# Attention with cosine similarity, 96 heads: the second pair's K squared and scaled in halves, no transposes by DMA, one dummy fewer, new orders on four engines

## The chip, the cores and the metric

The kernel runs on one core of a Trainium2 chip. What counts is the device time of one execution in microseconds (us), as the median of several runs. The engines are TensorE (PE, whose weight loads are listed as PEld), VectorE (DVE), ScalarE (ACT), GpSimd (POOL) and SyncE (SP), which here only issues DMAs. Each works through a list of its own in order, and they meet through semaphores.

## The reference

```
Q, K, V: (8, 12, 512, 64) float32;  tau = 0.1
Q_norm = Q / (norm(Q, axis=-1) + 1e-10)
K_norm = K / (norm(K, axis=-1) + 1e-10)
scores = einsum('bhqd,bhkd->bhqk', Q_norm, K_norm) / tau
weights = softmax(scores, axis=-1)
out = einsum('bhqk,bhkd->bhqd', weights, V)      float32
```

There are 8 x 12 = 96 heads, each with 512 queries and 512 keys of 64 numbers.

## The kernel before

Two heads form a pair, and the program is a loop over 48 pairs, numbered 0 to 47. Every step of a pair is put into a table with a name, an engine and the names of the steps it needs. The names are used below:

- LD.s.0 and LD.s.1 load Q and K of pair s (256 KB each), LV.s loads V, ST.s stores the result. All are issued by SP, but for the first K halves.
- SQ.s squares Q and K. Most pairs do this on POOL in one step of 1024 numbers per partition; pair 0 by quarters, pair 1 Q on ACT and K on DVE (512 each), pair 2 on POOL in two steps.
- SSQ.s adds the squares up in eight matmuls with an identity, and RED.s finishes this on DVE. Pair 0 does without the matmuls.
- The factor 1 / norm comes for pairs 0 to 2 from a logarithm and exponentials on ACT (LN.s, EX.s), later from small Newton steps on DVE (NEW.g.k, group g of one or two pairs).
- SCL.s.0 and SCL.s.1 multiply Q and K by these factors and write bf16 into `qn`; Q on DVE, K mostly on POOL.
- TR.s transposes `qn` on PE with an identity (16 small matmuls for a pair), and EVA.s copies the result from PSUM to `qt` on DVE. Pairs 0 and 1 do this in parts (TR.s.w, with w = 0 for Q and 1 for K). For seven pairs (9, 15, 21, 27, 33, 39, 45) K goes instead by a DMA that transposes, XT.s.1, which SP issues once SCL.s.1 is done; PE then transposes Q alone (8 matmuls), and the copy is half as wide.
- SCO.s.c computes the scores of a chunk of 128 keys for both heads (two matmuls of 512 columns) into one half of a PSUM tile of two halves, `scps`; EXP.s.c takes the exponential of the chunk on ACT (1024 numbers per partition), into `et`. So SCO may be at most two chunks ahead of EXP.
- VC.s turns V into bf16 on POOL, with a column of ones beside it. PV.s.h.t multiplies the exponentials with it (32 matmuls a pair); the column of ones gives the sum of the weights. RCP.s and NRM.s divide by it on DVE.

The buffers are rings: 18 pairs of `qk`, 6 of `vf`, 5 of `qn` and `qt`, 3 of `et`, 8 of `ob`. Several steps share three PSUM banks, named x, o0 and o1; who takes a bank waits for its last user by the order in PE's list.

The order of the work on each engine isn't decided by a planner: the table ORDER at the end of the file holds five written lists, one for each engine, and an engine does its list word for word. A step that waits holds up all that stands behind it on its engine. This counts on SP too: a store, a transposing DMA or a load into a ring place that isn't free yet holds up all loads behind it.

At the start PE has nothing to do until the first loads are there. It runs WARM = 19 dummy matmuls from the beginning, and FILL = (4, 0) more behind the first transposes (`fill`, line 639).

Of the kernel before, what the change touches and what calls it, by code (L numbers as in the profile page):

```python
# [5 lines left out]
ACT = mybir.ActivationFunctionType  # L6
# [118 lines left out]
def bass_cosine_similarity_attention_kernel(  # L125
# [127 lines left out]
    def sums(s, dst, free):  # L253

        sqs = [k for k in (("SQ", s, 0), ("SQ", s, 1)) if k in P.ops]
# [33 lines left out]
    def scaled(s, w, eng, r, needs):  # L289
        iqn, iq = s % R_QN, s % R_QK  # L290
        r = r.rearrange("p (h t) -> p h t", h=2).unsqueeze(3).to_broadcast([128, 2, NT, DIM])
# [3 lines left out]
        P.add(("SCL", s, w), eng, needs + [key("XT", p, w), key("TR", p), key("TR", p, w), *(key("TR", p, w, h) for h in range(2))],  # L295
              lambda e: e.tensor_tensor(out=o, in0=x, in1=r, op=ALU.mult))  # L296

    def transposed(s, name, blocks, dst, needs, **kw):
# [6 lines left out]
        P.add(name, "pe", needs + ["eye"], tr, **kw)  # L305

    def head():
# [13 lines left out]
        for h in range(2):  # L321
# [4 lines left out]
            for w in range(2):  # L326
# [4 lines left out]
                def tr(e, w=w, h=h, hs=hs):  # L331
# [6 lines left out]
                P.add(("EVA", 0, w, h), "dve", [("TR", 0, w, h)], lambda e, w=w, hs=hs: e.tensor_copy(  # L338
                    out=qt[0][hs, w], in_=tp[w][hs]))
# [80 lines left out]
    def pair(s):  # L420
# [14 lines left out]
        if s:  # L435
            gone = [key("RED", s - R_SQ, *y) for y in ((0,), (1,), (0, 0), (0, 1), (1, 0), (1, 1))]
            if s in SQ_ON:
                for w in range(2):
                    squares(s, engine(SQ_ON[s][w], "SQ", s, w), (w,), 512 * w, 512 * w + 512, [("LD", s, w)] + gone)
            else:  # L440
                squares(s, "pool", (0,), 0, 1024, [("LD", s, 0), ("LD", s, 1)] + gone)
        if 0 < s < LOGS:
# [7 lines left out]
                [("SCL", s - 1, 1)] if engine("pool", "SCL", s - 1, 1) == "dve" else [])  # L450
# [3 lines left out]
            scaled(s, 1, eng, r, [("EX", s, 0), ("EX", s, 1)])  # L454
# [42 lines left out]
        ready = [key("EVA", s), key("EVA", s, 0), key("EVA", s, 1), key("XT", s, 0), key("XT", s, 1)]  # L497
# [4 lines left out]
        for c in range(NT) if s else ():  # L502
# [14 lines left out]
            P.add(("SCO", s, c), "pe", [("SCO", *chunks[i - 1]) if i else None, *ready, scores_read(i - 2)], sco)  # L517
# [33 lines left out]
        for h in range(2) if s not in CHUNKED else ():  # L551
            for t in range(NT):
                def pv(e, h=h, t=t):
                    for c in range(NT):
# [10 lines left out]
                       *([("EVA", 1, 1), ("EVA", 0, 1, 1)] if s == 0 else [])], pv,  # L565
# [78 lines left out]
    if FILL[1]:  # L644
# [13 lines left out]
FILL = (4, 0)  # L658
# [10 lines left out]
        LD.0.0.0 LD.0.0.1 LD.1.0 LD.1.1 LD.2.0 LD.2.1 LD.3.0 LD.3.1 LV.0 LD.4.0 LD.4.1 LD.5.0 LD.5.1 LD.6.0 LV.1  # L669
        LD.6.1 LD.7.0 LD.7.1 LD.9.1 LD.9.0 LV.2 LV.3 LV.5 LD.8.1 LD.8.0 LV.4 LD.13.0 LD.15.0 LV.7 LD.11.1 LD.10.0  # L670
        LD.10.1 LD.11.0 LV.6 LV.8 LD.16.0 LD.14.1 ST.1 LD.12.0 LD.12.1 LD.13.1 LD.15.1 ST.4 XT.9.1 LD.18.0 LV.9
        LD.14.0 LV.10 LD.21.0 ST.0 LD.17.0 LV.14 LV.11 LD.16.1 LD.19.0 ST.5 ST.3 LD.24.0 LD.17.1 ST.2 LV.12 LV.15
        LD.18.1 LD.27.0 ST.6 LD.20.0 LV.13 LD.19.1 LD.23.0 LD.20.1 XT.15.1 LV.17 LV.16 LD.21.1 LD.24.1 LD.23.1 ST.7
# [167 lines left out]
```

## Time and profile before

| what | value |
|---|---|
| three timed runs | 191.36, 192.54, 193.3 us |
| their median | 192.54 us |
| the profiled execution | 191.03 us |
| its span, from the first to the last instruction | 189.2 us |
| granted TensorE clock | 1.000 |
| HBM read, written | 37.75 MB, 12.58 MB |
| DMA, mean over the span | 273 GB/s |

The page and the views of the trace describe the one profiled execution. An engine is busy while it computes; issuing DMAs and waiting on semaphores don't count. A group of instructions is given with its line in the code, engine and operation, then output and inputs, their shapes and the number of instructions; behind the bar its busy time in us, the mean duration of one in ns, and how long the engine was idle just ahead of such instructions and what ended that. Instructions of one engine overlap at their edges, so the mean duration is longer than the busy time divided by the count. Lines of the kernel before and after differ by up to 15 from the middle of the file on.

### The profile page before, as it was taken

To read this page: it belongs to the slowest core of one execution; us is meant where nothing else is said; L and a number is where in the kernel's file an instruction comes from. 1 tells how busy PE (TensorE), PEld (TensorE's weight loads), DVE (VectorE), ACT (ScalarE), POOL (GpSimd) and SP (SyncE) were. 2 spreads that over 40 slices of the span, in tenths; PEclk is the share of its full clock that TensorE was granted. 3 is DMA by queue.
4 is the path that set the end of the run, shared out by engine and by line. 5 is a ranking of instruction groups with operands and counts; after the bars stand their busy time and mean duration, and the time that the engine had idled before them with its cause. 6 is when DMAs were issued, how large, how long until landed. Compare 5 with 4: busy or idle time off the path is not lost.

```text
span 189.2 us, 7234 instructions
## 1 busy us (share of the span) xinstructions
PE 174.0 (92%) x3023; PEld 110.2 (58%) x3023; DVE 146.1 (77%) x451; ACT 181.3 (96%) x209; POOL 160.1 (85%) x147
## 2 busy tenths in 40 slices
PE   7999998999998999998898999999999999988893
PEld 5455664665665565665565656565656666654542
DVE  2999988879887977878798688876869877697424
ACT  5599999999999999999999999999999999999992
POOL 1599999999999999999999999999899998355100
PEclk9999999999999999999999999999999999999999
DMA  5999999579999999999999999999999570938423
GB/s 151 335 349 349 348 350 368 175 234 310 361 359 251 309 353 346 314 254 349 376 373 303 241 343 299 352 255 281 294 318 328 132 243 22 309 90 170 132 93 116
DMA packets 56257, 51.73 MB, mean 273 GB/s; under 512 B 6944, under 2 KB 56224, under 8 KB 56224
## 3 DMA queue, kind: packets, MB, share of 16 engines
q1 hardware_dynamic: 55792, 50.93, 86.4%
q8 instruction: 24, 0.39, 0.9%
q10 hardware_dynamic: 432, 0.33, 0.6%
q14 instruction: 9, 0.07, 0.1%
HBM read 37.75 MB, written 12.58 MB: 266 GB/s over the span
## 4 chain that ended last, share of the span: by engine, by line
ACT 84%; PE 6%; DVE 4%; POOL 2%; DMA 2%; issue 0%; ACTq 0%; DVEq 0%
ACT et L527 80%; ACT et L523 2%; DMA qk<-in_K_dram 2%; PE bps L268 2%; PE scps L512 1%; POOL qn L296 1%; PE scps L359 1%; POOL sq L250 1%; DVE qt L490 1%; PE bps L555 1%; PE bps L484 1%; DVE qn L296 1%; DVE qn L327 1%; ACT et L364 1%; PE bps L333 0%
## 5 line engine op out<-in xcount | busy, mean ns | idle before, releaser
L527 ACT ACTIVATE et<-scps 128x1024 bf16<-128x1024 f32 x184 | 168.9, 1168 | 0.2 <-PE scps L512 0.2
L250 POOL TENSOR_TENSOR sq<-qk 128x1024 bf16<-128x1024 f32 (+2 forms) x48 | 87.3, 1830 | 6.0 <-DMA qk<-in_Q_dram 5.7
L512 PE MATMUL scps<-qt 64*128 64x512 bf16 x376 | 74.1, 386 | 8.5 <-ACT et L527 7.2
L555 PE MATMUL bps<-vb,et 128*128 128x65 bf16 x1472 | 66.4, 194 | 0.0
L555 PEld LDWEIGHTS bps<-vb,et 128*128 128x128 bf16 x1472 | 51.8, 98 | 24.5 <-issue 16.2
L296 POOL TENSOR_TENSOR qn<-qk,rk 128x512 bf16<-128x512 f32 x44 | 45.3, 1042 | 9.4 <-DVE rk L398 5.7
L490 DVE COPY qt<-bps 128x1024 bf16<-128x1024 bf16 (+1 forms) x46 | 29.9, 650 | 10.9 <-PE bps L484 10.0
L296 DVE TENSOR_TENSOR qn<-qk,nps 128x512 bf16<-128x512 f32 x50 | 33.8, 681 | 0.5
L571 DVE TENSOR_TENSOR ob<-bps,rd 128x512 f32<-128x512 f32 x47 | 32.5, 692 | 1.1
L512 PEld LDWEIGHTS scps<-qt 64*128 64x128 bf16 x376 | 18.3, 93 | 25.9 <-ACT et L527 14.3
L268 PE MATMUL bps<-sq,ident 128*128 128x128 bf16 x376 | 29.1, 220 | 0.5 <-POOL qn L296 0.5
L532 POOL TENSOR_SCALAR vb<-vf 128x512 bf16<-128x512 f32 x48 | 29.5, 625 | 0.0
L268 PEld LDWEIGHTS bps<-sq,ident 128*128 128x128 bf16 x376 | 21.1, 98 | 11.0 <-issue 8.1
L569 DVE RECIPROCAL rd<-bps 128x8 f32<-128x8 f32 x47 | 9.7, 207 | 18.7 <-PE bps L555 15.2
L484 PE MATMUL bps<-ident,qn 64*128 64x64 bf16 x680 | 17.9, 191 | 1.4 <-DVE nps L276 0.3
L484 PEld LDWEIGHTS bps<-ident,qn 64*128 64x128 bf16 x680 | 13.2, 95 | 7.8 <-DVE nps L276 3.4
L276 DVE TENSOR_REDUCE nps<-bps 128x16 f32<-128x128 f32 x45 | 13.4, 297 | 2.1 <-PE bps L268 2.1
L390 DVE TENSOR_TENSOR nps<-nps,ys 128x32 f32<-128x32 f32 (+1 forms) x48 | 9.1, 192 | 1.0
L394 DVE SCALAR_TENSOR_TENSOR nps<-nps,ys 128x32 f32<-128x32 f32 (+1 forms) x48 | 9.1, 191 | 0.7
L237 PE MATMUL scps<-warm_in 128*128 128x256 bf16 x23 | 4.8, 394 | 1.1 <-DVE warm_in L232 1.1
L398 DVE SCALAR_TENSOR_TENSOR nps<-nps,ys 128x16 f32<-128x16 f32 (+1 forms) x25 | 4.3, 177 | 0.5
L402 DVE TENSOR_SCALAR ys<-nps 128x32 int32<-128x32 int32 (+1 forms) x24 | 4.4, 181 | 0.4
(45 smaller groups left out, 46.8 us busy)
## 6 DMA issues: line engine op xcount, KB each, us to landing
vf<-in_V_dram SPq DMA_DIRECT2D x48, 256.0 KB, 5.4
qk<-in_Q_dram SPq DMA_DIRECT2D x47, 256.0 KB, 5.9
qk<-in_K_dram SPq DMA_DIRECT2D x47, 256.0 KB, 6.0
out_dram<-ob SPq DMA_DIRECT2D x47, 256.0 KB, 4.5
qk<-in_Q_dram SPq DMA_DIRECT2D x2, 128.0 KB, 2.6
qk<-in_K_dram ACTq DMA_DIRECT2D x2, 128.0 KB, 2.8
out_dram<-ob SPq DMA_DIRECT2D x1, 128.0 KB, 2.3
qt<-qn SPq DMA_TRANSPOSE x7, 3.5
```

The source lines that it names most:

```text
L250: emit = lambda e: e.tensor_tensor(out=b, in0=a, in1=a, op=ALU.mult)
L268: last = e.matmul(out=ps[:, 0:128], lhsT=ident[:, :], rhs=sq[s % R_SQ][:, :, 8 * k : 8 * k + 8], start=(k == 0), stop=(k == 7))
L276: lambda e: e.tensor_reduce(out=dst(None), in_=ps[:, 0:128].rearrange("p (w g e) -> p w g e", w=2, e=8), axis=AX.X, op=ALU.add))
L296: lambda e: e.tensor_tensor(out=o, in0=x, in1=r, op=ALU.mult))
L484: last = e.transpose(t_ps[:, k, b, :], qn[s % R_QN][ks, b // NT, b % NT].rearrange("p h d -> p (h d)"), ident[ks, ks])
L490: lambda e, lo=lo, hi=hi: e.tensor_copy(out=qt[iqt][:, :].rearrange("p w t (k x) -> p k (w t) x", k=2)[:, :, lo:hi], in_=t_ps[:, :, lo:hi]))
L512: last = e.matmul(out=sc_ps[:, 2 * b + k, :], lhsT=qt[iqt][64 * h : 64 * h + 64, 1, n, :], rhs=qt[iqt][64 * h : 64 * h + 64, 0, :, :], sta ...
L527: lambda e, c=c, b=b: e.activation(out=et[iet][:, c, :, :], in_=sc_ps[:, 2 * b : 2 * b + 2, :], func=ACT.Exp, scale=scale, bias=bias))
L532: lambda e: e.tensor_scalar(out=vb[:, iq, :, :, 0:DIM].rearrange("p c h d -> p h c d"), in0=vf[iv][:, :, :].rearrange("p h (c d) -> p h c ...
L555: last = e.matmul(out=o_ps[:, h, 65 * t : 65 * t + 65], lhsT=et[iet][:, c, h, 128 * t : 128 * t + 128], rhs=vb[:, iq, c, h, :], start=(c = ...
L569: lambda e: e.reciprocal(out=rd[io][:, :], in_=grid[:, :, :, DIM]))
L571: lambda e: e.tensor_tensor(out=ob[io][:, :], in0=grid[:, :, :, 0:DIM], in1=rd[io][:, :].unsqueeze(3).to_broadcast([128, 2, NT, DIM]), op= ...
```

## The change

There are five edits.

1. K of pair 1 is squared in two steps, one for each head: the first head (256 numbers per partition) on DVE as SQ.1.1.0, the second on ACT as SQ.1.1.1, right behind Q's square. Before, DVE did all 512. SSQ.1 needs all three.
2. K of pair 1 is scaled (SCL.1.1.0, SCL.1.1.1), transposed (TR.1.1.0, TR.1.1.1) and copied (EVA.1.1.0, EVA.1.1.1) in two halves of 256 keys. The second half uses the bank o0. The chunks SCO.1.0 and SCO.1.1 need the first half of K alone, SCO.1.2 and SCO.1.3 the second too.
3. No pair is transposed by DMA any more (`XT = {}`); PE transposes Q and K of all pairs, in 16 matmuls, with the copy of full width.
4. FILL goes from (4, 0) to (3, 0): three late dummies.
5. The lists of SP, POOL, DVE and PE are new. ACT's list is as before but for SQ.1.1.1.

```diff
-        sqs = [k for k in (("SQ", s, 0), ("SQ", s, 1)) if k in P.ops]
+        sqs = [k for k in (("SQ", s, 0), ("SQ", s, 1), ("SQ", s, 1, 0), ("SQ", s, 1, 1)) if k in P.ops]
...
-    def scaled(s, w, eng, r, needs):
+    def scaled(s, w, eng, r, needs, part=(), ts=slice(0, NT)):
         iqn, iq = s % R_QN, s % R_QK
...
-        o = qn[iqn][:, w].rearrange("p t h d -> p h t d")
-        x = qk[iq][:, w].rearrange("p h (t d) -> p h t d", t=NT)
+        o = qn[iqn][:, w, ts].rearrange("p t h d -> p h t d")
+        x = qk[iq][:, w].rearrange("p h (t d) -> p h t d", t=NT)[:, :, ts]
...
+    def copied(name, needs, dst, src_):
+
+        eng = engine("dve", *name)
+        P.add(name, eng, needs, (lambda e: e.activation(out=dst, in_=src_, func=ACT.Copy)) if eng == "act"
+              else lambda e: e.tensor_copy(out=dst, in_=src_))
...
     def second():
 
-        tp = [b[:, 0:256].bitcast(bf16).rearrange("p (t x) -> p t x", t=NT) for b in (x_ps, o_ps[:, 1])]
-        for w in range(2):
-            transposed(1, ("TR", 1, w), range(NT * w, NT * w + NT), tp[w],
-                       [("SCL", 1, w)] + ([("RED", 1, 0)] if w else []),
-                       take=["o1" if w else "x"], until=("EVA", 1, w))
-            P.add(("EVA", 1, w), "dve", [("TR", 1, w)],
-                  lambda e, w=w: e.tensor_copy(out=qt[1][:, w], in_=tp[w]))
+        banks = {"x": x_ps, "o1": o_ps[:, 1], "o0": o_ps[:, 0]}
+        for w, j, bank in ((0, None, "x"), (1, 0, "o1"), (1, 1, "o0")):
+            lo, hi = (0, NT) if j is None else (2 * j, 2 * j + 2)
+            tp = banks[bank][:, 0:256].bitcast(bf16).rearrange("p (t x) -> p t x", t=NT)[:, 0 : hi - lo]
+            part = (w,) if j is None else (w, j)
+            transposed(1, ("TR", 1, *part), range(NT * w + lo, NT * w + hi), tp,
+                       [("SCL", 1, *part)] + ([("RED", 1, 0)] if j == 0 else []) + ([("TR", 1, 1, 0)] if j else []),
+                       take=[bank], until=("EVA", 1, *part))
+            copied(("EVA", 1, *part), [("TR", 1, *part)], qt[1][:, w, lo:hi], tp)
...
-            P.add(("SCO", s, c), "pe", [("SCO", *chunks[i - 1]) if i else None, *ready, scores_read(i - 2)], sco)
+            P.add(("SCO", s, c), "pe", [("SCO", *chunks[i - 1]) if i else None, *ready, key("EVA", s, 1, 1) if c > 1 else None,
+                                      scores_read(i - 2)], sco)
...
-SQ_ON = {1: ('act', 'dve'), 2: ('pool', 'pool')}
+SQ_ON = {1: (('act',), ('dve', 'act')), 2: (('pool',), ('pool',))}
...
-XT = {9: (1,), 15: (1,), 21: (1,), 27: (1,), 33: (1,), 39: (1,), 45: (1,)}
+XT = {}
...
-FILL = (4, 0)
+FILL = (3, 0)
...
     "act": """
-        LD.0.1.0 LD.0.1.1 table SQ.0.0.0 SQ.0.1.0 SQ.0.1.1 LN.0.0 EX.0.0 LN.0.1 EX.0.1 SQ.1.0 EXP.0.0.0 EXP.0.0.1 LN.1
+        LD.0.1.0 LD.0.1.1 table SQ.0.0.0 SQ.0.1.0 SQ.0.1.1 LN.0.0 EX.0.0 LN.0.1 EX.0.1 SQ.1.0 SQ.1.1.1 EXP.0.0.0
...
```

How the lists move is seen at three places. The first is DVE's row at the start of the program, from the scaling of pair 0's first head on. In it `qn0` and `qt0` belong to pair 0, `sq1`, `xs1` and `qn1` to pair 1, `xs2` to pair 2; the lines with `COPY qt0` are EVA.0. Before:

```order
L327 TENSOR_TENSOR qn0<-qk0,bps 128x4x64 x2
L318 TENSOR_REDUCE xs0<-sq0 128x4
L338 COPY qt0<-bps 64x512
L327 TENSOR_TENSOR qn0<-qk0,nps 128x4x64
L338 COPY qt0<-bps 64x512
L250 TENSOR_TENSOR sq1<-qk1 128x512
L327 TENSOR_TENSOR qn0<-qk0,nps 128x4x64
L338 COPY qt0<-bps 64x512
L276 TENSOR_REDUCE xs1<-bps 128x16
L338 COPY qt0<-bps 64x512
L296 TENSOR_TENSOR qn1<-qk1,nps 128x2x4x64 x2
L276 TENSOR_REDUCE xs2<-bps 128x16
```

The same stretch of DVE's row after the change:

```order
L333 TENSOR_TENSOR qn0<-qk0,bps 128x4x64 x2
L324 TENSOR_REDUCE xs0<-sq0 128x4
L311 COPY qt0<-bps 64x512 x2
L333 TENSOR_TENSOR qn0<-qk0,nps 128x4x64
L250 TENSOR_TENSOR sq1<-qk1 128x256
L333 TENSOR_TENSOR qn0<-qk0,nps 128x4x64
L311 COPY qt0<-bps 64x512
L276 TENSOR_REDUCE xs1<-bps 128x16
L311 COPY qt0<-bps 64x512
L296 TENSOR_TENSOR qn1<-qk1,nps 128x2x2x64
L296 TENSOR_TENSOR qn1<-qk1,nps 128x2x4x64
L296 TENSOR_TENSOR qn1<-qk1,nps 128x2x2x64
```

The two copies of the first head stand side by side, where a scaling of the second head stood between them; the square is half as wide; and K of pair 1 is scaled in two pieces around Q.

The second place is PE's row in the same stretch; `sq1`, `sq2` and `sq3` mark the sums of pairs 1 to 3, `qt0` and `qt1` the scores of pairs 0 and 1, `warm_in` the dummies. Before:

```order
L333 MATMUL bps<-ident,qn0 64x128 x8
L237 MATMUL scps<-warm_in 128x256 x4
L333 MATMUL bps<-ident,qn0 64x128 x4
L359 MATMUL scps<-qt0 128x512 x3
L268 MATMUL bps<-sq1,ident 128x128 x8
L333 MATMUL bps<-ident,qn0 64x128 x4
L359 MATMUL scps<-qt0 128x512 x3
L268 MATMUL bps<-sq2,ident 128x128 x8
L301 MATMUL bps<-ident,qn1 128x128 x8
L359 MATMUL scps<-qt0 128x512 x2
L512 MATMUL scps<-qt1 128x512 x2
L268 MATMUL bps<-sq3,ident 128x128 x8
```

PE's row after the change:

```order
L339 MATMUL bps<-ident,qn0 64x128 x8
L237 MATMUL scps<-warm_in 128x256 x3
L366 MATMUL scps<-qt0 128x512 x2
L339 MATMUL bps<-ident,qn0 64x128 x4
L268 MATMUL bps<-sq1,ident 128x128 x8
L339 MATMUL bps<-ident,qn0 64x128 x4
L366 MATMUL scps<-qt0 128x512 x4
L301 MATMUL bps<-ident,qn1 128x128 x2
L268 MATMUL bps<-sq2,ident 128x128 x8
L301 MATMUL bps<-ident,qn1 128x128 x4
L366 MATMUL scps<-qt0 128x512 x2
L526 MATMUL scps<-qt1 128x512 x2
```

Two scores of pair 0 now stand ahead of the second head's transposes, and the transposes of pair 1 stand in pieces: half of K ahead of the sums of pair 2, Q behind them, the other half of K further down.

The third place is SP's row around the first transposing DMA, XT.9.1, with the buffers' numbers (`qk` 0 to 17, `vf` 0 to 5, `ob` 0 to 7). Before:

```order
L429 DMA qk12<-in_K_dram 128x2x256
L429 DMA qk13<-in_K_dram 128x2x256
L429 DMA qk15<-in_K_dram 128x2x256
L575 DMA out_0_dram<-ob4 128x2x256
L475 DMA_TRANSPOSE qt4<-qn4 128x4x128
L429 DMA qk0<-in_Q_dram 128x2x256
L432 DMA vf3<-in_V_dram 128x2x256
L429 DMA qk14<-in_Q_dram 128x2x256
```

After the change, the stretch of SP's row with the first stores:

```order
L436 DMA qk16<-in_K_dram 128x2x256
L436 DMA qk15<-in_Q_dram 128x2x256
L439 DMA vf3<-in_V_dram 128x2x256
L436 DMA qk15<-in_K_dram 128x2x256
L436 DMA qk4<-in_K_dram 128x2x256
L590 DMA out_0_dram<-ob3 128x2x256
L590 DMA out_0_dram<-ob5 128x2x256
```

Before, loads of pairs 14 and 18 stand behind the transposing DMA of pair 9 and behind the store of pair 4; after, all loads up to pair 16 and one of pair 22 stand ahead of the first store, and there is no transposing DMA.

More of the change, by code (lines that the diff above doesn't have):

```diff
@@ L438, in pair @@
                 for w in range(2):
-                    squares(s, engine(SQ_ON[s][w], "SQ", s, w), (w,), 512 * w, 512 * w + 512, [("LD", s, w)] + gone)
+                    n = len(SQ_ON[s][w])
+                    for h in range(n):
+                        lo = 512 * w + 512 // n * h
+                        squares(s, SQ_ON[s][w][h], (w, h) if n > 1 else (w,), lo, lo + 512 // n, [("LD", s, w)] + gone)
             else:
@@ L449, in pair @@
             free = [("SCL", 0, 0, 1), ("SCL", 0, 1, 1)] if s == 1 else [("SCL", s - 1, 0)] + (
-                [("SCL", s - 1, 1)] if engine("pool", "SCL", s - 1, 1) == "dve" else [])
+                [k for k in (("SCL", s - 1, 1), ("SCL", s - 1, 1, 0), ("SCL", s - 1, 1, 1)) if k in P.ops]
+                if engine("pool", "SCL", s - 1, 1) == "dve" else [])
             for w, dst in ((0, rq), (1, r)):
@@ L453, in pair @@
             scaled(s, 0, "dve", rq, [("EX", s, 0), ("EX", s, 1)])
-            scaled(s, 1, eng, r, [("EX", s, 0), ("EX", s, 1)])
+            for j in range(2) if s == 1 else ():
+                scaled(1, 1, eng, r, [("EX", 1, w) for w in range(2)], (j,), slice(2 * j, 2 * j + 2))
+            if s > 1:
+                scaled(s, 1, eng, r, [("EX", s, w) for w in range(2)])
         elif s:
```

273 lines of the change are left out of this document (137 added, 136 removed).

## The prediction

> **What bounds the kernel now.** I read the page's busy line first, then the groups of instructions, then ACT's waits, then the chain that ended last, and then the start and the tail instruction by instruction. The page has:
>
> ```profile
> span 189.2 us, 7234 instructions
> PE 174.0 (92%) x3023; PEld 110.2 (58%) x3023; DVE 146.1 (77%) x451; ACT 181.3 (96%) x209; POOL 160.1 (85%) x147
> ...
> L527 ACT ACTIVATE et<-scps 128x1024 bf16<-128x1024 f32 x184 | 168.9, 1168 | 0.2 <-PE scps L512 0.2
> ```
>
> ACT works for 181.3 of 189.2 us, and ahead of its 184 large exponentials it idles 0.2 us in all. Their cost is 168.9 / 184 = 0.918 us each, since successive ones overlap (a single one shows 1168 ns). Neither their number nor their size is in the diff. The chain of waits agrees; its columns are start, length and what ran:
>
> ```profile
> 28.79 0.62 PE bps L268 x8
> 29.41 0.34 PE scps L512 x2
> ...
> 29.77 152.28 ACT et L527 x166
> 182.05 3.84 ACT et L523 x5
> ```
>
> From 29.77 to 185.89 us the chain is ACT alone: 166 exponentials in 152.28 us, 0.917 us each. So the change can act at three places only: ahead of 29.77, after 185.89, or by making ACT wait (or wait less) in between, where there is 0.2 us to win at most in this execution. ACT's idle time shows the start (waiter, cause, us in total, times, longest):
>
> ```profile
> ACT xl L282 <- DVE xs L318: 1.1, 1, 1.1
> ACT et L364 <- PE scps L359: 0.6, 1, 0.6
> ...
> ACT xl L282 <- DVE xs L276: 0.2, 1, 0.2
> ACT et L527 <- PE scps L512: 0.2, 1, 0.2
> ```
>
> The 1.1 us belongs to the first pair's norms, whose steps up to there the change leaves alone. The 0.6 us ahead of the first exponential and the 0.2 us ahead of the second pair's logarithm are what it touches.
>
> **The start, step by step.** The timeline of the first 14 us, columns start, length, engine and line:
>
> ```profile
> 1.10 4.23 PE L237 MATMUL scps<-warm_in 128*128 128x256 bf16 x19 [1.10 <-DVE warm_in L232]
> ...
> 3.35 1.25 ACT L248 ACTIVATE sq<-qk 128x256 bf16<-128x256 f32 x3 [0.35 <-DMA qk<-in_Q_dram]
> ...
> 6.03 0.41 DVE L338 COPY qt<-bps 64x512 bf16<-64x512 bf16 x1
> ...
> 6.18 0.61 PE L237 MATMUL scps<-warm_in 128*128 128x256 bf16 x4
> ...
> 6.60 0.42 DVE L327 TENSOR_TENSOR qn<-qk,nps 128x256 bf16<-128x256 f32 x1 [0.17 <-ACT nps L286]
> 6.63 0.63 ACT L248 ACTIVATE sq<-qk 128x512 bf16<-128x512 f32 x1
> ...
> 6.94 0.41 DVE L338 COPY qt<-bps 64x512 bf16<-64x512 bf16 x1
> ...
> 7.32 0.69 DVE L250 TENSOR_TENSOR sq<-qk 128x512 bf16<-128x512 f32 x1
> ...
> 7.42 0.82 PE L359 MATMUL scps<-qt 64*128 64x512 bf16 x3
> ...
> 7.84 1.08 ACT L364 ACTIVATE et<-scps 128x512 bf16<-128x512 f32 x2 [0.58 <-PE scps L359]
> ...
> 8.12 2.03 POOL L250 TENSOR_TENSOR sq<-qk 128x512 bf16<-128x512 f32 x2 [2.19 <-DMA qk<-in_Q_dram]
> ...
> 8.17 0.62 PE L268 MATMUL bps<-sq,ident 128*128 128x128 bf16 x8
> ...
> 9.15 0.22 ACT L282 ACTIVATE xl<-xs 128x16 f32<-128x16 f32 x1 [0.23 <-DVE xs L276]
> ...
> 9.62 1.92 ACT L364 ACTIVATE et<-scps 128x1024 bf16<-128x1024 f32 x2
> ...
> 10.38 1.89 POOL L250 TENSOR_TENSOR sq<-qk 128x1024 bf16<-128x1024 f32 x1 [0.22 <-DMA qk<-in_K_dram]
> ...
> 10.91 0.28 DVE L276 TENSOR_REDUCE xs<-bps 128x16 f32<-128x128 f32 x1
> ...
> 11.42 0.21 ACT L282 ACTIVATE xl<-xs 128x16 f32<-128x16 f32 x1
> ...
> 12.02 1.02 ACT L364 ACTIVATE et<-scps 128x1024 bf16<-128x1024 f32 x1
> ...
> 13.53 0.41 PE L484 MATMUL bps<-ident,qn 64*128 64x64 bf16 x16
> ```
>
> First scores. They need the copies of the first head's Q and K. The second copy (6.94) now comes right behind the first: DVE's steps of this size follow each other by 6.94 − 6.60 = 0.34 us, so it starts at 6.37 and ends at 6.78; PE followed the copy by 7.42 − 7.35 = 0.07, so the scores start at 6.85 instead of 7.42. The dropped dummy (0.61 / 4, at most 0.15) lies ahead of that and costs nothing to leave out: three dummies end by about 6.65. The Q copy is no longer what the first exponential waits for; ACT is. After its 512-wide square (to 7.26) it now has a second, 256-wide one. K's load is there by 7.32, when DVE squares it; the three 256-wide squares took 1.25, 0.42 each, so ACT is free at 7.74. First exponential: 7.74 instead of 7.84, a gain of 0.1.
>
> Second pair's logarithm. Its sums on PE (8.17) wait for all squares. DVE's half now starts at the same 7.32 and takes about 0.42 (the multiply of that size at 6.60), ACT's half ends at 7.74 too, so PE starts at 7.80: 0.37 earlier, and the logarithm at 9.15 − 0.37 = 8.78; ACT has by then ended its two exponentials (7.74 + 1.08 = 8.82). The next exponential (9.62) needs on PE the sums (0.62), four transposes, and two scores; they end about 9.35. So it gains 0.27.
>
> There the gain meets two things that don't move. The third pair's logarithm (11.42) waits for POOL's squares, which wait for a load until 8.12; they end at 10.15, and DVE's sum at 10.91 + 0.28 = 11.19. ACT can start the logarithm at 11.22, not before: the gain shrinks to 0.2, and 12.02 becomes 11.82. Then the fourth pair's squares (10.38, again released by a load) hold the third pair's transposes at 13.53. The scores behind these additionally wait for the copy of the second half of pair 1's K, which stands behind two small steps on DVE. The first load of V goes behind one more load of K: loads land 0.75 us apart (8.12 and 10.38 are the first and the last of four), so about 11.9 instead of 11.1, and POOL takes it up only after the squares that end at 12.27; price 0, with 0.4 us of cover. In all I keep 0.15 of the start, between 0 and 0.3. Even that can be lost at 28.79 us, where a PE group sets the chain: if PE and POOL ahead of it don't move, ACT only waits longer there. That is the lower bound 0.
>
> **The tail.** The last matmuls and the last normalisations change places.
>
> ```profile
> 185.88 0.16 DVE L626 RECIPROCAL rd<-bps 128x2 f32<-128x2 f32 x1
> ...
> 185.93 0.30 PE L612 MATMUL scps<-vb,et 128*128 128x65 bf16 x4 [0.19 <-ACT et L523]
> ...
> 186.47 0.29 DVE L628 TENSOR_TENSOR ob<-scps,rd 128x128 f32<-128x128 f32 x1
> 186.68 0.28 DVE L628 TENSOR_TENSOR ob<-bps,rd 128x128 f32<-128x128 f32 x1
> ```
>
> Four matmuls of the last group (of its eight, the four that read earlier exponentials) move behind the group ahead of it; PE had 0.19 idle ahead of 185.93, which covers all but a few hundredths. On DVE the normalisation of 0.28 now stands ahead of the last reciprocal, in a gap of about 0.2 after 186.04. Cost 0 to 0.2; I take 0.1.
>
> **The seven DMA transposes.** They become eight more PE transposes each, and a copy twice as wide on DVE. The waits of the DMA-issuing queue, and the windows:
>
> ```profile
> SPq L475 <- POOL vb L532: 14.5, 4, 4.8
> SPq L475 <- POOL qn L296: 8.3, 3, 2.9
> ```
> ```profile
> 25.00:180.00 155.00, 145.31 (x2649) 92.88 (x2647) 123.07 (x375) 154.84 (x170) 141.45 (x127) 1.00 0.90 278
> 35.00:40.00 5.00, 4.76 (x90) 3.09 (x88) 3.25 (x9) 5.00 (x7) 5.00 (x4) 1.00 0.51 151
> ```
>
> PE: sixteen transposes take 0.41, so eight add at most 0.21, seven times 1.4 us. Between 25 and 180 us PE idles 155 − 145.3 = 9.7 us, DVE 32 us. That covers it in sum: 0. What goes with them: the queue stood 14.5 + 8.3 = 22.8 us waiting to issue these seven, with every load behind them held up (in 35 to 40 us the DMA engines are at 0.51 of their time). In this execution no load comes late for it: the 0.2 us of ACT are all there is. So its worth in this sum is 0. [...]
>
> The searched orders elsewhere leave the same number of exponentials, in the same row on ACT. POOL's row is the same up to its 25th operation. Gain at most the 0.2 us of idle time; loss bounded below.
>
> **The sum.** 189.2 − 0.15 + 0.1 = 189.15 us of span; the profiled execution lasted 191.03, 1.83 more than its span, so 191.0. The three timed runs lie above it: 191.36, 192.54, 193.3, the median 1.5 us more. This spread has no row; whatever lengthens those runs must make ACT wait. The held-up loads and PE's tightness are the candidates. Loads no longer held up take away some, from 0 to 1.5; I take half, 0.75 (a choice). Forecast: 191.0 + 0.75 = 191.7 us.
>
> **The rivals.** (A) Nothing that counts moves: the start's gain is lost at 28.79, and the spread is not from loads. Then 191.03 + 1.5 = 192.5. For it: no mid-run wait for a load. Against: the queue's 22.8 us.
>
> (B) All of the spread goes with the held-up loads, and the start keeps its 0.3: 190.7. For it: the 0.51 window. Against: the same absence of a late load.
>
> (C) Slower: PE becomes the bound around the seven pairs. PE's 9.7 us of idle time over 42 pairs (155 / 3.67, four exponentials each) are 0.23 per pair, and 0.21 more work comes to seven of them, with the new order setting other groups close together. If a pair's added work shows in full on ACT, with the copy behind it on DVE (0.3, half of a copy of 0.65):
>
> ```profile
> L490 DVE COPY qt<-bps 128x1024 bf16<-128x1024 bf16 (+1 forms) x46 | 29.9, 650 | 10.9 <-PE bps L484 10.0
> ```
>
> it is 0.5 per pair, 3.5 for seven: 191.0 + 3.5 = 194.5. It decides where PE has less than 0.21 idle in a pair's 3.67 us. Against it: the 39 pairs that were transposed on PE alone already show 0.2 us of ACT's wait together.
>
> (D) PE's pace. The 19 early dummies take 4.23 us, 0.22 each; the four late ones 0.61, at most 0.15 each, so PE was faster by 6.2 us. With fewer dummies that could come later; if it came only after the first scores and sums (0.82 and 0.62), these would take up to twice as long, 1.4 us more: 191.0 + 1.4 = 192.4. [...]
>
> **The numbers.** Chances: forecast 0.4, A 0.25, B 0.15, C 0.15, D 0.05. The three timings lie 1% apart, so 1% is what can be told. Faster by over 1% means under 190.6: half of B and a little of the forecast, 0.11. Slower by over 1% means over 194.5: half of C and its like, 0.11. Within: 0.78. The range 190.5 to 193.8 leaves out a third of B and most of C.
>
> **What would show it.** Right: the first exponential at 7.7 to 7.75, the exponential of line 364 that was at 12.02 at about 11.8; ACT's idle time before the large exponentials still under 0.5 us; no queue waits for transposes; the span near 189.1. A: 12.02 moves, but the ACT-only part of the chain starts later than 29.77 with more wait. C: ACT waiting for PE's scores several times, near pairs 9, 15, 21 and so on. D: the transposes at 5.50 or the scores at about 6.85 at twice their spacing. Wrong outright: a POOL or DVE wait for a load after 15 us, or a span under 188.5.

## The result, and the profile after

| | before | after |
|---|---|---|
| timed runs side by side, 17 each, median | 191.87 us | 191.32 us |
| lowest | 190.98 us | 190.49 us |
| middle half of the runs | 191.57 to 192.20 us | 191.14 to 191.47 us |
| the profiled execution | 191.03 us | 191.23 us |
| its span | 189.2 us | 189.4 us |

The ratio is 0.9964, with a 95% interval of 0.9946 to 0.9981. The gain of some 0.55 us is clear of the noise and under 1%; the forecast was 191.7 us. Yet the two profiled executions stand the other way round: the one after is 0.2 us longer. The median of before, 192.54 us over three runs, came out at 191.87 over 17, and its profiled execution, 191.03 us, is quicker than all but one of these 17.

The page after, busy times and ACT's large exponentials (busy time and mean ns, then the idle time ahead of them):

```profile
span 189.4 us, 7341 instructions
PE 174.1 (92%) x3078; PEld 110.7 (58%) x3078; DVE 148.1 (78%) x453; ACT 181.7 (96%) x210; POOL 160.7 (85%) x147
...
L542 ACT ACTIVATE et<-scps 128x1024 bf16<-128x1024 f32 x184 | 169.1, 1128 | 0.5 <-PE scps L526 0.4
```

The seven transposes are on PE now: 3078 matmuls instead of 3023, which is seven times eight more and one dummy less. PE's busy time grew by 0.1 us only. ACT's idle time ahead of the exponentials went from 0.2 to 0.5 us. All of the 0.4 us that PE causes lies at one place, which the chain of waits shows (start, length, what ran):

```profile
24.88 0.63 DVE ob L586
25.52 0.25 DVE nps L276
25.82 0.41 PE bps L498 x16
26.44 0.59 PE bps L570 x16
27.03 0.38 PE scps L526 x2
27.40 0.60 PE bps L570 x16
28.00 0.32 PE scps L526
28.32 0.32 issue
28.64 0.40 PE scps L526
29.06 130.32 ACT et L542 x142
159.41 22.11 ACT et L542 x24
181.57 0.60 PE scps L526 x2
```

From 12.0 to 29.06 us the end was set by DVE and PE in turn, and from there to 181.5 us by ACT alone. Behind that the chain runs through PE's last groups and DVE's last normalisations, while ACT computes on to 186.26 us. Before, it was ACT's to 185.89 us. Between two matmuls of one score group stands a stop of PE of 0.32 us that waits for nothing recorded ("issue"). The start, row by row:

```profile
3.48 1.20 ACT L248 ACTIVATE sq<-qk 128x256 bf16<-128x256 f32 x3 [0.50 <-DMA qk<-in_Q_dram]
...
5.64 1.06 PE L339 MATMUL bps<-ident,qn 128*64 128x128 bf16 x8 [0.30 <-DVE qn L333]
...
7.21 0.60 PE L366 MATMUL scps<-qt 64*128 64x512 bf16 x2
...
7.64 1.08 ACT L371 ACTIVATE et<-scps 128x512 bf16<-128x512 f32 x2
...
9.07 0.22 ACT L282 ACTIVATE xl<-xs 128x16 f32<-128x16 f32 x1 [0.35 <-DVE xs L276]
...
9.62 1.94 ACT L371 ACTIVATE et<-scps 128x1024 bf16<-128x1024 f32 x2
...
11.91 1.00 ACT L371 ACTIVATE et<-scps 128x1024 bf16<-128x1024 f32 x1
...
12.81 1.93 ACT L542 ACTIVATE et<-scps 128x1024 bf16<-128x1024 f32 x2
```

ACT's first square, which waits for a load, began 0.13 us later than before (3.48 against 3.35). The eight transposes took 1.06 us, where the same eight took 0.74 before, so PE was still at its slow pace (they follow each other by some 107 ns, before mostly by 56). Still the first exponential came 0.2 us earlier. The tail, the last store in the two timelines, before and then after:

```profile
186.79 0.35 ACTq L632 DMA_DIRECT2D out_dram<-ob  x1
```
```profile
187.18 0.35 ACTq L647 DMA_DIRECT2D out_dram<-ob  x1
```

ACT's last exponential ended at 184.78 + 1.09 = 185.87 before and at 184.26 + 2.00 = 186.26 after:

```profile
184.26 2.00 ACT L538 ACTIVATE et<-scps 128x1024 bf16<-128x1024 f32 x3
```

From there the last store is issued after 0.92 us in both. What also differs is the load side. The page's row of the DMA engines, in 40 slices of 4.7 us, before and after:

```profile
DMA  5999999579999999999999999999999570938423
```
```profile
DMA  6999999999469999999999959899959500754435
```

Before, the DMA engines slacken in slices 8 and 9 (33 to 42 us), around the first transpose, which the queue issued at 35.40 us:

```profile
35.40 1.30 SPq L475 DMA_TRANSPOSE qt<-qn  x1
```

After, they are full to 47 us and slacken only then. The loads run further ahead. The queue stands longer than before, but now at its V loads and stores, which follow POOL and DVE (V loads behind POOL: 31.6 us against 15.2):

```profile
SPq L439 <- POOL vb L547: 31.6, 14, 9.8
SPq L590 <- DVE ob L586: 15.5, 4, 7.1
```

### The profile page after: what moved, and what is told of

Read it like the earlier page. It is cut to its first block, busy times and chain, and to the rows that moved or that the text cites. A ratio compares the mean times of both kernels' runs of the same rounds, so it can differ in the third digit from the quotient of the medians.

```text
span 189.4 us, 7341 instructions
## 1 busy us (share of the span) xinstructions
PE 174.1 (92%) x3078; PEld 110.7 (58%) x3078; DVE 148.1 (78%) x453; ACT 181.7 (96%) x210; POOL 160.7 (85%) x147
## 4 chain that ended last, share of the span: by engine, by line
ACT 82%; DVE 7%; PE 7%; DMA 1%; issue 1%
ACT et L542 80%; PE scps L526 2%; DMA qk<-in_Q_dram 1%; DVE qn L296 1%; PE bps L570 1%; DVE ob L586 1%; DVE qt L504 1%; ACT et L371 1%; PE bps L339 1%; PE bps L558 1%; DVE nps L276 1%; PE bps L268 1%; DVE ob L643 1%; PE bps L498 0%; DVE xs L324 0%
## 5 line engine op out<-in xcount | busy, mean ns | idle before, releaser
L570 PE MATMUL bps<-vb,et 128*128 128x65 bf16 x1472 | 65.1, 194 | 0.2
L296 POOL TENSOR_TENSOR qn<-qk,rk 128x512 bf16<-128x512 f32 x44 | 45.8, 1051 | 11.8 <-DVE rk L405 11.7
L504 DVE COPY qt<-bps 128x1024 bf16<-128x1024 bf16 x46 | 31.8, 691 | 10.1 <-PE bps L498 9.4
L296 DVE TENSOR_TENSOR qn<-qk,nps 128x512 bf16<-128x512 f32 (+1 forms) x51 | 33.9, 671 | 0.8 <-ACT nps L286 0.2
L498 PE MATMUL bps<-ident,qn 64*128 64x64 bf16 x736 | 18.8, 191 | 2.4 <-DVE ob L586 0.4
L498 PEld LDWEIGHTS bps<-ident,qn 64*128 64x128 bf16 x736 | 14.2, 95 | 9.8 <-DVE nps L276 4.0
```

The source lines that it names most:

```text
L498: last = e.transpose(t_ps[:, k, b, :], qn[s % R_QN][ks, b // NT, b % NT].rearrange("p h d -> p (h d)"), ident[ks, ks])
L504: lambda e, lo=lo, hi=hi: e.tensor_copy(out=qt[iqt][:, :].rearrange("p w t (k x) -> p k (w t) x", k=2)[:, :, lo:hi], in_=t_ps[:, :, lo:hi]))
L570: last = e.matmul(out=o_ps[:, h, 65 * t : 65 * t + 65], lhsT=et[iet][:, c, h, 128 * t : 128 * t + 128], rhs=vb[:, iq, c, h, :], start=(c = ...
```

## The experiments

Every ratio is to the kernel before, run on the same chip in the same stretch, with its 95% interval.

### Parts of the change apart

Four kernels take the start (K of pair 1 in two steps, the dummies, and the rows of PE and DVE as far as the scores of pair 2), the transposes by DMA, and the rows behind the start in other combinations. In the first the new start runs with the old rest:

```diff
 the start: as changed, up to SCO.2.0 on PE and EVA.2 on DVE
-XT = {}
+XT = {9: (1,), 15: (1,), 21: (1,), 27: (1,), 33: (1,), 39: (1,), 45: (1,)}
 rows behind the start, POOL's and SP's rows: as before
```

> The kernel after in its start alone: K of pair 1 in halves, three late dummies and the new rows of PE and DVE up to the scores SCO.2.0 and the copy EVA.2; everything behind that, the transposing DMAs and the queue's row as before. Loads: 1.000. Start: about 0.9965 to 0.9985 (0.3 to 0.7 us), the exponential that was at 12.02 at 11.8 to 11.9. Orders: 1.000.

In the second the old start runs with the new rest:

```diff
 the start: as before
-XT = {9: (1,), 15: (1,), 21: (1,), 27: (1,), 33: (1,), 39: (1,), 45: (1,)}
+XT = {}
 rows behind the start, POOL's and SP's rows: as changed
```

> The other way round: the start as before (K of pair 1 whole, four late dummies, the old rows up to SCO.2.0 and EVA.2), the rest in the new orders, no transposing DMAs. Loads: about 0.9965. Start: 1.000. Orders: about 0.9965; with xt_gone at 1.000 that would be the orders and not the loads.

In the third only the seven transposes leave the kernel before:

```diff
-XT = {9: (1,), 15: (1,), 21: (1,), 27: (1,), 33: (1,), 39: (1,), 45: (1,)}
+XT = {}
...
-XT.9.1 LD.18.0 LV.9 LD.14.0
+LD.18.0 LV.9 LD.14.0
```

> The kernel before with nothing changed but the seven transposing DMAs, which are gone; PE transposes K of those pairs too, at the place in its row where it transposed Q. Loads (held-up loads made the runs long): ratio about 0.9965, no waits of the DMA queue for transposes, runs closer together. Start (the gain is made in the first 13 us): 1.000. Orders (the gain is in the new order of the rest): 1.000, or a little over 1 if PE's added work shows.

The fourth has that and the new start, with the old rows behind it:

> The new start and no transposing DMAs, but the old orders behind SCO.2.0 and EVA.2 and the old row of the DMA queue. Loads: about 0.9965, as xt_gone. Start: as start_alone. Orders: 1.000. If the parts add up: xt_gone times start_alone.

| start | seven transposes | rows behind | median | ratio |
|---|---|---|---|---|
| old | by DMA | old | (before) | 1 |
| new | by DMA | old | 191.66 us | 0.9993 (0.9968 to 1.0018) |
| old | on PE | old | 193.36 us | 1.0083 (1.0051 to 1.0116) |
| new | on PE | old | 192.32 us | 1.0029 (1.0009 to 1.0048) |
| old | on PE | new | 192.30 us | 1.0018 (0.9994 to 1.0043) |
| new | on PE | new | 191.32 us | 0.9964 (0.9946 to 0.9981) |

The last row is the comparison above, from other runs than the four ahead of it; its repetition below gives 0.9954. No part alone makes the kernel faster. The theory of held-up loads had foretold 0.9965 for the old start with the old rows and no transposes by DMA, which measured 1.0083. Taking the transposes off the DMA queue costs 0.8% with the old start and 0.4% with the new one (1.0029 against 0.9993). The new rows, searched for the kernel without these transposes, give that back and more: 0.65% (1.0083 to 1.0018, and 1.0029 to 0.9964). The new start gives 0.54% in both pairs without transposes by DMA, and 0.07%, within the error, beside them. Each of these differences is uncertain by 0.3 to 0.4%.

Where the new rows gain is seen from the trace of each kernel, in three stretches: to the first exponential of pair 9, from there to the last exponential's end, and the rest of the span. These times are counted in ACT's records (pair 9, the first that was transposed by DMA, begins with the 33rd of the 184 large exponentials), in us:

```
kernel                                    to pair 9   on to ACT's end   to the span's end
before                                      42.53         143.34             3.34
old rows, no transposes by DMA              45.07         144.08             3.24
new start, old rows, transposes by DMA      43.32         145.00             3.47
new start, old rows, none                   42.97         144.51             3.22
old start, new rows                         43.42         143.55             2.96
after                                       42.71         143.54             3.12
```

From pair 9 on the new rows take 143.5 us, with either start. The old rows take between 143.3 and 145.0, and the profile of before is the quickest of the four; the other three are altered, so that part of their time may be misfit. In the new rows ACT waits for no scores in this stretch. In the three altered kernels with the old rows its waits there sum to 0.3, 1.2 and 0.6 us, in the order of the table; the rest of their longer time is not explained. What a slower execution of the old rows is made of shows in the new start with the old rest, whose profiled execution is the longest of its 12 (193.62 us). POOL's timeline there, with its idle time in brackets:

```profile
51.70 1.89 POOL L250 TENSOR_TENSOR sq<-qk 128x1024 bf16<-128x1024 f32 x1 [1.10 <-DMA qk<-in_K_dram]
```
```profile
75.59 1.89 POOL L250 TENSOR_TENSOR sq<-qk 128x1024 bf16<-128x1024 f32 x1 [0.98 <-DMA qk<-in_K_dram]
```

ACT's timeline behind these, where it waits for scores that come late on PE:

```profile
55.91 22.12 ACT L542 ACTIVATE et<-scps 128x1024 bf16<-128x1024 f32 x24 [0.25 <-PE scps L526]
78.53 1.94 ACT L542 ACTIVATE et<-scps 128x1024 bf16<-128x1024 f32 x2 [0.50 <-PE scps L526]
```

And the queue's own waits from 30 to 62 us (in total, times, longest):

```profile
SPq L489 <- POOL vb L547: 3.5, 1, 3.5
SPq L489 <- POOL qn L296: 2.9, 1, 2.9
```

L489 is the transposing DMA: the queue stood 6.4 us for two of them, and loads of K that it issued some 8 us behind each came 1 us late. These are the late loads for which the prediction had no row. That the standing queue made them late is argued only: in before it stood as long for the same transposes, and no load came late. In the trace of after, POOL waits for no load behind 15 us. But the transposes' wait is not the only cause of the slower rows: without any, the altered old rows still take 144.1 and 144.5 us.

Part of what the seven transposes cost on the engines can be seen in these two kernels. In both, ACT waits for scores behind the copies of pairs 9, 33 and 39 (0.45 us in all, in each). These are copies that the change makes twice as wide: 0.69 us, where before they took 0.42. The chain of waits with the old start leaves ACT at the copy of pair 39 so:

```profile
152.13 0.70 DVE qt L490
152.88 0.67 PE bps L555 x16
153.91 31.42 ACT et L527 x34
```

PE stands 0.22 us for the copy, and ACT 0.21 us for the scores behind it. In before ACT doesn't wait there. These 0.45 us are less than the 0.7 and 1.6 us that the ratios give; what makes up the rest is not shown.

### The change again, and its start

The changed kernel as it is was run once more, on another chip.

> The kernel after once more, beside the next three on the same chip: 0.9964 again, 0.994 to 0.999.

191.24 us, ratio 0.9954 (0.9925 to 0.9983): the same gain. Its profiled execution took 193.36 us, with PE's clock at half pace from 8.8 to 15.6 us; from pair 9 on it took 143.63 us to ACT's end, as the others with the new rows.

To see whether ACT or PE sets the end in the start, one more square of 512 numbers was put on ACT ahead of the first exponential (its output goes nowhere):

```diff
-SQ.1.0 SQ.1.1.1 EXP.0.0.0
+SQ.1.0 SQ.1.1.1 XSQ EXP.0.0.0
```

> The kernel after with one more square of 512 numbers on ACT, into a tile nobody reads, ahead of the first exponential: ACT is 0.52 us late there (512-wide squares follow each other so). If the start passes on in full: 0.5 us more than after_again, 0.27%. If it is taken up on the way (by the third pair's squares at 11.2 us, the fourth's at 13.5, or the stop at 28.4): under 0.2 us, 0.1%.

191.43 us, ratio 0.9977 (0.9941 to 1.0012), against 191.24 us and 0.9954 for the unaltered one beside it. The added 0.52 us cost 0.2 us by the medians and 0.4 by the ratios, whose intervals overlap: the times don't settle it. The profile speaks for some slack on ACT, though the added square (L652) stands in its chain of waits:

```profile
7.54 0.52 ACT extra L652
8.06 0.97 ACT et L371 x2
...
11.74 1.28 DVE qn L296 x2
...
28.37 0.40 PE scps L526
28.80 23.94 ACT et L542 x26
```

The kernel of the next experiment, on the same chip, lacks the square. Its logarithm of the second pair began 0.22 us earlier (8.70 against 8.92), its large exponentials 0.10 us earlier (12.44 against 12.54), and those of pair 5 at 27.38 us in both. ACT's first square had itself begun 0.11 us earlier there. So in these two profiles nothing of the 0.52 us is left by pair 5. Behind 11.7 us the chain runs through DVE and PE.

The loads were to be thinned out ahead of 28 us, by letting those of pairs 12 to 17 wait for the squares six pairs ahead:

```diff
+                      + ([("SQ", s - 6, 0)] if 12 <= s < 18 else []),
```

> The kernel after, but loads of pairs 12 to 17 are issued only after the squares of the pair six before, so that the DMA engines are not full from 19 to 28 us. In all profiles but one PE stops at about 28.4 us at the same place of its row (matmul 345 to 347) without a semaphore it waits for, and goes on about 1.3 us after a 16 KB instruction fetch ends. If that stop is a late instruction fetch behind the loads: gone, ACT's wait there 0.4 us less, ratio to before 0.1 to 0.5% under after_again. If it is a wait of another kind: unchanged. If late loads count: slower.

191.21 us, ratio 0.9951 (0.9920 to 0.9982), as without. The DMA engines were at 1.10 of their time from 20 to 24 us and at 1.06 from 24 to 28, so the edit didn't do what it was for, and this run settles nothing about the loads.

### PE's stop near 28 us

In 12 of the 14 profiles PE stops near 28 us, whatever instruction stands there: in before ahead of a group of sums of squares, in after in the middle of a score group. Counting matmul records from the program's first, the stop always stands behind record 345, 346 or 347. To tell a count from a place in the work, the changed kernel did the sixteen transposes of pair 3 twice over, at about 18 us:

```diff
-                    for b in range(lo, hi):
+                    for b in list(range(lo, hi)) * (2 if s == 3 else 1):
```

> The changed kernel, with the sixteen transposes of pair 3 done twice over (same inputs, same result): 16 more matmuls, 0.41 us more for PE at about 17 to 20 us. If PE's stop near 28 us comes from its instructions being fetched: it stays at matmul record 343 to 349 counted from the program's first, so 16 matmuls earlier in the row of work, some 0.7 us earlier in time, and again 1.2 to 1.7 us behind the end of a fetch. If it belongs to the work (a wait that the records don't show): it moves to record 359 to 365 with the instruction that it stands ahead of. Time: 0.995 to 0.998, since ACT waits for PE little there.

PE's timeline there, with the added transposes (32 in a row instead of 16) and the stop:

```profile
17.97 0.64 PE L498 MATMUL bps<-ident,qn 64*128 64x64 bf16 x32
...
28.81 0.96 PE L570 MATMUL bps<-vb,et 128*128 128x65 bf16 x15 [1.30 <-issue]
```

The stop stayed at record 345. It now stands in the weighted sum ahead of the score group, 16 matmuls earlier in the work. Beside it, the last transfer on the DMA queue named "instruction" (16 KB each, from the trace's DMA records) that ended ahead of the stop, in us:

```
kernel                              transfer ends   PE stops   PE goes on   stop   from transfer's end
before                                  27.49         28.32      28.79      0.47         1.30
after                                   27.40         28.32      28.64      0.32         1.24
after, pair 3 transposed twice          27.39         27.50      28.81      1.30         1.42
after, loads thinned out                27.96         28.06      29.35      1.29         1.39
after, transposes put back (below)      28.44         28.45      29.71      1.27         1.28
before, no transposes by DMA            28.49         28.34      29.99      1.65         1.50
new start, old rows, none               26.32       no stop
```

PE goes on 1.24 to 1.50 us behind the transfer's end, so how long it stood goes by when it stopped and when the transfer ended. The six other profiles with the stop fit too (1.31 to 1.61 us). The two without one reached record 346 some 1.2 and 2.0 us behind the transfer's end, about as late as PE goes on in the others, or later. That the stop hangs on the count of instructions is shown by the count, which held against a move of the work; that it hangs on this transfer is read from the steady step behind it. That the transfer brings PE its next instructions is read from the queue's name; no row says whose they are. Why the transfer is early or late (the DMA engines were at 1.10 of their time from 24 to 28 us in before and in after) is argued only.

Three of the long stops were followed by something worse. The windows of the altered kernel, with the granted clock third from the end, and then those of before without transposes by DMA:

```profile
28.00:32.00 4.00, 3.19 (x41) 2.12 (x43) 1.58 (x5) 1.81 (x3) 4.00 (x5) 0.61 1.11 350
32.00:36.00 4.00, 3.65 (x83) 2.37 (x77) 3.30 (x11) 4.00 (x5) 1.61 (x3) 0.96 1.09 347
```
```profile
28.00:32.00 4.00, 2.28 (x40) 1.35 (x40) 2.13 (x6) 2.63 (x4) 4.00 (x5) 0.94 1.09 360
32.00:36.00 4.00, 3.92 (x56) 2.24 (x53) 2.63 (x10) 3.20 (x4) 1.96 (x3) 0.63 0.60 207
```

Counted at half pace, the clocks below 1.00 in these windows make 3.4 us in each, behind a stop of 1.30 and of 1.65 us (and 0.87 and 0.70 in the same windows, 3.4 us again, in the kernel with the transposes put back, behind one of 1.27 us), and ACT was busy for only 1.81 and 2.63 of 4 us from 28 us on. In the kernel with thinned loads a stop of 1.29 us brought no such stretch, with a clock of 1.00 in all windows up to 185 us.

In time the doubled transposes measured 191.83 us, ratio 1.0002 (0.9982 to 1.0022), outside what was expected: it is 0.4 to 0.5% above the changed kernel's 0.9964 and 0.9954, some 0.7 to 0.9 us, uncertain by 0.5 to 0.7, for 0.23 us of work (the 32 took 0.64 us, the sixteen of after 0.41). So PE has hardly any slack ahead of 29 us. Whether the longer stop, or the slow stretch behind it, adds to the cost is not told apart; nine of the 12 runs show a clock of 0.999 or 1.000, so a slow stretch in some of them doesn't make the median.

### The transposes by DMA in the new rows

First the seven were put back into the changed kernel, at places of the queue chosen from its order alone:

```diff
-XT = {}
+XT = {9: (1,), 15: (1,), 21: (1,), 27: (1,), 33: (1,), 39: (1,), 45: (1,)}
...
-LV.22 LV.17 LD.23.1 ST.10
+LV.22 LV.17 LD.23.1 XT.15.1 ST.10
```

> The kernel after with the seven transposing DMAs put back for K of pairs 9, 15, 21, 27, 33, 39 and 45, between the stores of its own queue row; all else as after. PE saves 56 transposes (at most 1.4 us). If the held-up loads cost time (my prediction): 0.3 to 0.4% slower than after, ratio about 1.000. If the transposes on PE cost time (xt_gone alone was 1.0083): 0.3 to 0.8% faster than after, 0.989 to 0.993. If neither counts in the new orders: as after_again.

200.62 us, ratio 1.0434 (1.0386 to 1.0481). The timeline of the queue and of ACT around the second of them:

```profile
63.98 1.86 SPq L489 DMA_TRANSPOSE qt<-qn  x1
...
70.86 1.02 ACT L542 ACTIVATE et<-scps 128x1024 bf16<-128x1024 f32 x1 [5.71 <-PE scps L526]
```

It was issued at 63.98 us, behind V loads that waited for POOL, and ACT stood 5.71 us for the scores that need it. The places were bad, so this is no price of the transposes themselves. They were then put where, in the trace of after, the queue takes up its next entry once their input is done:

```diff
-LD.20.1 LV.15 LV.18
+LD.20.1 LV.15 XT.15.1 LV.18
```

> The changed kernel with the seven transposes by DMA put back, each at the place of the queue where its input is done in the changed kernel's trace, so that it waits for little; the later eight transposes on PE and half of the copy on DVE fall away. If a transpose by DMA costs only where the queue stands for it: ratio within 0.001 of the changed kernel's 0.995 to 0.996, ACT's idle time before the large exponentials within 0.3 us of its 0.5. If it relieves PE in a way that counts: 0.990 to 0.993. If the transfers themselves or their issue hold up the loads: above 0.999, with queue waits for POOL under 1 us each.

193.59 us, ratio 1.0073 (1.0039 to 1.0107), still 1.1% above the changed kernel. PE's waits in that profile, and then the DMA issues of before and of this kernel (median us from issue to landing in the last column):

```profile
PE scps L526 <- DMA qt<-qn: 2.6, 3, 1.5
```
```profile
qt<-qn SPq DMA_TRANSPOSE x7, 3.5
```
```profile
qt<-qn SPq DMA_TRANSPOSE x7, 5.7
```

The median one takes 5.7 us to land, against 3.5 before, and PE waits 2.6 us for three of them. The same transfer took longer where the DMA engines were full: the four that took 5.7 us and more had them at 1.10 to 1.22 of their time while they were under way, and the ten others, before and here, at 0.30 to 0.91, but for one of 4.5 us at 1.20. Its profiled execution also had a stop of 1.27 us at record 345 and a stretch at half pace behind it, so not all of the 1.1% need be the transposes'. The six runs with a clock of 0.999 or 1.000 have a median of 192.51 us, still 0.4% above before.

### The rows of one queue alone

To see whether the gain is the queue's row (loads with more lead) or the compute rows, the two were exchanged. First the new queue row over the old rows:

```diff
 the start: as changed; XT = {}
 rows behind the start, POOL's row: as before
 SP's row: as changed, but LD.37.1 LV.33 LV.38 LV.43 LV.44 up to six places earlier
```

> The new start, no transposes by DMA, the old rows on PE, DVE and POOL behind the start, and the new row of the DMA queue (five loads stand up to six places earlier, since these rows need them). With the old queue row this mix measured 1.0029. Theory L (the gain lies in the queue's row: loads come with more lead): 0.994 to 0.998. Rival C (the gain lies in the compute rows, which place the seven pairs' added transposes): 1.001 to 1.005, as with the old queue row. DMA share at 36 to 40 us: full under both, since that follows from the row itself.

Then the old queue row under the new rows:

```diff
 all but SP's row: as changed
 SP's row: as before without XT, but LD.38.1 LV.36 LD.43.0 LD.43.1 ST.26 ST.27 LV.40 LD.47.1 up to eight places earlier
```

> The changed kernel with the old row of the DMA queue, without its seven transposes (eight entries stand up to eight places earlier, all behind pair 33). Theory L: the gain goes, 1.000 to 1.005, with POOL or DVE waiting for loads somewhere between 40 and 170 us. Rival C: the gain stays, 0.994 to 0.997, and no wait for a load after 15 us.

235.14 us, ratio 1.2247 (1.2212 to 1.2281), and 232.00 us, 1.2100 (1.2056 to 1.2145). Neither theory is told from the other: both mixes fail in the same way. The queue's waits in the first and in the second:

```profile
SPq L439 <- POOL vb L547: 73.7, 15, 15.6
```
```profile
SPq L439 <- POOL vb L547: 76.3, 13, 21.6
```

A V load stands in the queue for a buffer that POOL frees later in the other kernel's row, everything behind it stands too, and ACT ends up waiting 38.8 us for PE (38.3 in the second). The two kinds of rows fit only together.

## Why the prediction was right, and where it wasn't

**What bounds the kernel.** Right from 29 us on: ACT's exponentials are what they were, and follow each other without a wait to the end, though from 181.5 us the chain goes through PE and DVE. The prediction counted the start's steps on ACT, with PE at 28.79 us as a bound. In the profile after, ACT is in the chain up to 12.0 us, and DVE and PE from there to 29.06. Added work on PE came through; what of added work on ACT comes through the times don't settle, and in the profile nothing was left at pair 5.

**The start.** The first exponential came at 7.64, 0.1 us ahead of the forecast of 7.74. The second pair's logarithm came at 9.07 instead of 8.78, and the exponential behind it at 9.62 as before: the forecast took PE's durations from before, where it was at full pace from 5.5 us (transposes 56 ns apart), and here it was so from 6.8 us (107 ns apart until then). The later steps kept 0.11 us (11.91 against 12.02; forecast 11.82) and 0.13 at 12.81 against 12.94. This is less than the start varies between executions: in the other profiles the large exponentials began at 12.93 and 13.54 with the old start, and with the new one at 12.44 to 13.37, or at 14.76 and 15.40. By pair 5 this is gone in the profile (27.64 us against 27.60), as the lower bound at 28.79 said: PE and DVE ahead of it didn't move. The timed runs give the new start 0.54%, some 1.0 us, where the transposes are gone. No profile shows where that arises, and it stays open.

**The tail.** Sized at 0.1 us, it measured nothing: 0.92 us from ACT's end to the last store's issue in both.

**The seven transposes.** "Zero in the sum" was the step that failed most plainly. The idle times of PE (9.7 us) and DVE (32 us) were counted as sums and found large enough; taken away under the old rows the transposes cost 0.4 to 0.8%. In part that is because the wider copies fall where the old rows have no room: PE stands for three of the seven, and ACT behind it (0.45 us in all). It is rival C, with a smaller size, and through DVE's copy more than through PE's matmuls. From pair 9 on the old rows without the transposes took 0.74 us more in the profile than before, 0.1 per transposed pair and not 0.5. Nearly all of the 2.5 us by which this profile was late at pair 9 came with PE's stop at 28 us and the slow stretch behind it. With the new rows ACT waits at no such place, so that C doesn't show after the change.

**The half of the spread.** The forecast of 191.7 lies 0.4 us above the measured 191.32, but that is in part luck. It stands on the profiled execution of before, 191.03, and on half of a spread of 1.5 us that three runs gave; over 17 runs before itself came down to 191.87, from which 191.7 would be a gain of 0.2 and not of 0.55. The reason given was half right at most. Late loads behind standing transposes do occur in a longer execution of the old rows (two of 1 us, in one profile), and the middle half of the runs narrowed from 0.63 to 0.33 us. But the transposes' removal isn't what gives it: without the new rows it costs. The gain comes with rows that fit the kernel without transposes, 0.65% (some 1.2 us) by two comparisons; in the profiles 0.5 and 1.0 us of it lie from pair 9 on. Between the two profiles of before and after the change looks like a loss of 0.2 us.

**The other rivals.** A (nothing moves) and B (all spread goes) lie outside: the lowest run moved by 0.49 us, the median by 0.55. D's mechanism is there with either start. In the trace of before the dummies follow each other by 213 ns up to 4.9 us and by 109 from 6.3 us on. By such spacings PE reached full pace between 4.1 and 7.1 us in the profiles with the new start, and between 4.2 and 5.5 us in the three with the old. The changed kernel's second profile, in which the pace fell back from 8.8 to 15.6 us (mean clock 0.982), took 193.36 us; two of the 17 runs after, with mean clocks of 0.988 and 0.989, took 193.40 and 193.56 us, and have no profile. Since it varies so much with one and the same start, it looks like a matter of the execution and not of the change, but the dummy left out had no run of its own.

What the runs leave open: whether the queue's row or the compute rows carry the gain, what delays the transfer behind which PE goes on near 28 us, what the seven transposes cost beyond the 0.45 us, and where the start's 0.5% arises.

## What to carry to other kernels

A hand-written or searched order belongs to one set of operations: an edit tried under the old order can show the misfit and not the edit, here 0.4 to 0.8% for seven transposes, and over 20% for one queue's row alone. Ask engine by engine, in each stretch of time, whether it has room; an idle time summed over the run covers nothing. And compare the profiled execution with the spread of the timed runs before building a sum on it, since one trace of a kernel with a spread of 1% may be one of its luckiest.

## What the runs showed of the hardware

- PE stopped at the same count of its instructions, behind matmul record 345 to 347, for 0.3 to 1.65 us, and went on 1.2 to 1.6 us behind the end of a 16 KB transfer on the queue named "instruction" (12 of 14 profiles). Sixteen small matmuls put in earlier moved the stop to another instruction, and it lasted 1.30 us instead of 0.32.
- Behind PE stops of 1.27, 1.30 and 1.65 us the clock went below 1.00 for what counts as 3.4 us at half pace (0.70, 0.61 and 0.63 in the lowest window of 4 us), and behind one of 1.29 us it stayed at 1.00.
- Transposing DMAs of the same size landed after 3.5 us in one order and after 5.7 in another (medians of seven). The four that took 5.7 us and more had the DMA engines at 1.10 to 1.22 of their time, nine of the ten others at 0.30 to 0.91. Each held the queue for 1.2 to 2.0 us while it was issued, where a load took some 0.5 (median in before).
